# Cached keys laid out feature-major by the host, split straight from SBUF instead of transposed on TensorE

## The chip, the cores and the metric

The kernel runs on one core of one Trainium2 chip. The metric is the device time of one launch in microseconds (us). The profiled execution is one launch taken by the hardware profiler; its rows give times on the engines: PE (TensorE matmuls), PEld (weight loads of TensorE), DVE (VectorE), ACT (ScalarE), POOL (GpSimd) and SP (SyncE, which here only issues DMAs).

## The reference

One step of a one-layer hybrid encoder, for a prompt of 2048 tokens and for 8 batches of 16 new tokens with cached state. A combined projection feeds three branches (forgetting attention "fox" with 8 heads of 64, retention, and attention into 256 memory tokens with 4 heads of 128), which are gated, projected and merged. The change touches how the cached keys of the 8 batches enter the scores:

```python
PAST_LEN, DEC_BATCH, DEC_SEQ = 2048, 8, 16
# cache_fox_k (1, 8, 2048, 8, 64), cache_mem_k (1, 8, 256, 4, 128)
def fox_attend(q, c_q, q_pos, k, v, c_k):
    s = jnp.einsum('bqhd,bkhd->bhqk', q, k) * (DH_FOX ** -0.5)
    s = s + jnp.swapaxes(c_q, 1, 2)[..., :, None] - jnp.swapaxes(c_k, 1, 2)[..., None, :]
    s = jnp.where(k_pos[None, :] <= q_pos[:, None], s, -jnp.inf)
    p = jax.nn.softmax(s, axis=-1)
    return jnp.einsum('bhqk,bkhd->bqhd', p, v)
def memory_attend(q, mk, mv):
    s = jnp.einsum('bthd,bmhd->bhtm', q, mk) * (DH_MEM ** -0.5)
    return jnp.einsum('bhtm,bmhd->bthd', jax.nn.softmax(s, axis=-1), mv)
```

## The kernel before

Every fp32 operand of a matmul is split into a rounded part `h` and a rest `l`, both of a type that TensorE takes in one pass, and a product is three matmuls (`mm3`: h*h, h*l, l*h). The helper `split` does it with one cast on ACT (line 202) and one subtraction on DVE (line 205):

```python
S.copy(h, src)
V.tensor_tensor(l, src, f32(h), ALU.subtract)
```

The program has a long projection (to about 1700 us), then two lanes woven together, then the output blocks (from about 2850 us). The right lane does the prompt's retention and then the prompt's fox attention. The left lane does the memory attention of the prompt (`mem_prompt`), of the 8 batches (`decode_mem`), the fox attention of the 8 batches (`decode_fox`) and the first output block. Both lanes are generators, and `weave` and `paced` mix them in a fixed ratio as the program is written out; a scheduler with a model of each instruction's time then settles the order on each engine. On the chip every engine works its list off in that order, and SP issues all loads and stores from a single queue, so an instruction that waits holds up those behind it on its engine.

The prompt's fox attention runs beside everything that is told here. For a block of 128 queries and up to 512 keys, PE makes scores in `sc` (lines 1315 to 1318), DVE takes the maximum `f_mx` (1322), ACT the exponential `pt` (1323), POOL scales `pt` (1327) by a factor `f_f` that DVE makes (1247), PE transposes `pt` into the PSUM tile `tp` (1349), ACT and DVE split that into `ph` and `pl`, and PE multiplies with the values into `ov` (1367, 1368).

`decode_fox` takes one batch at a time (`unit(b)`), two batches overlapping. A batch has four score blocks (`ci`, 512 keys each) and one for the 16 new keys. In each of the four, SP loads two pieces `dkt` of 512 KB: keys on the partitions, 512 features in a row. For each group `g4` of 128 features PE transposes four 128x128 pieces of them into a bank of `tp` (line 1487), `split` makes `dkh` and `dkl` from that bank, and three matmuls add to the scores `ys`. So a batch has 64 transposes and 16 splits of 512 columns, all 8 have 512 and 128. Buffers: three of `dkt`, three of `dkh` and of `dkl`; the three banks of `tp` are shared with the prompt's attention. The cached values `dvt` are split by POOL alone (`dvh` line 1529, `dvl` line 1530) and multiplied into `ym`.

`decode_mem` does the same on a small scale: per batch one load `mkt` of 512 KB, 16 transposes (line 1646), two splits into `mkh` and `mkl`, and 12 matmuls into `ys`; the values are split by ACT (`mvh`) and POOL (`mvl`). It runs beside the end of retention, which loads a state `st` for each batch, splits it into `sth` and `stl`, and stores it back.

Of the kernel before, what the change touches and what calls it, by code (L numbers as in the profile page):

```python
# [9 lines left out]
F32 = mybir.dt.float32  # L10
# [9 lines left out]
P = 128  # L20
# [3 lines left out]
NB, TS = 8, 16  # L24
# [48 lines left out]
def body(ctx: ExitStack, tc: tile.TileContext, a, o, stop=99):  # L73
# [25 lines left out]
    def ptp(dt=F32):  # L99
        return ps["tp"].tile([P, 512], dt, name="tp")  # L100
# [10 lines left out]
    def pdt(dt=F32):  # L111
        return ps["tp"].tile([P, 512], dt, name="tp")
# [70 lines left out]
    def dma(out, in_):  # L183
        nc.sync.dma_start(out, in_)
# [1207 lines left out]
    def decode_fox(dp, dw):  # L1392
# [56 lines left out]
        def unit(b):  # L1449
# [17 lines left out]
            kv = a["cache_fox_k"][b].rearrange("(p j) c -> p j c", p=P)  # L1467
# [7 lines left out]
            for ci in range(5):  # L1475
                sc = pys()
                if ci < 4:
                    w = 512
                    kts = []
                    for j in range(2):  # L1480
                        kt = dw.tile([P, 2, 512], F32, name="dkt", bufs=3)
                        dma(kt, kv[:, 4 * ci + 2 * j:4 * ci + 2 * j + 2])
                        kts += [kt[:, 0], kt[:, 1]]
                    for g4 in range(4):
                        p = pdt()
                        for j in range(4):
                            T.transpose(p[:, j * P:(j + 1) * P], kts[j][:, g4 * P:(g4 + 1) * P], ident)
                        kh = dw.tile([P, 512], F32R, name="dkh", bufs=3)
                        kl = dw.tile([P, 512], F32R, name="dkl", bufs=3)
                        split(kh, kl, p)  # L1490
                        mm3(sc, qb[0][:, g4], qb[1][:, g4], kh, kl, g4 == 0, False)
                    T.matmul(sc, selr[32 * ci:32 * ci + 16], crow[32 * ci:32 * ci + 16], start=False, stop=True)
                else:
                    w = 16
                    bs = slice(b * TS, (b + 1) * TS)
                    for g4 in range(4):
                        mm3(sc[:, :16], qb[0][:, g4], qb[1][:, g4], ks[0][:, g4, bs], ks[1][:, g4, bs], g4 == 0, False)
                    T.matmul(sc[:, :16], selr[:16], cnT[:, bs], start=False, stop=False)
                    T.matmul(sc[:, :16], identb, dmask, start=False, stop=True)
# [114 lines left out]
    def decode_mem(dp, dw):  # L1614
# [14 lines left out]
        def unit(b):  # L1629
            bs = slice(b * TS, (b + 1) * TS)  # L1630
            kt = dw.tile([P, 2, 512], F32, name="mkt")
            vt = dw.tile([P, 2, 512], F32, name="mvt")
            dma(kt, a["cache_mem_k"][b].rearrange("(m p) c -> p m c", p=P))
# [6 lines left out]
            parts = []  # L1640
            for h2 in range(2):
                p = ptp()
                for hh in range(2):
                    for m in range(2):
                        h = 2 * h2 + hh
                        T.transpose(p[:, (2 * hh + m) * P:(2 * hh + m + 1) * P], kt[:, m, h * P:(h + 1) * P], ident)
                kh = dw.tile([P, 512], F32R, name="mkh", bufs=3)
                kl = dw.tile([P, 512], F32R, name="mkl", bufs=3)
                split(kh, kl, p)
                parts.append((kh, kl))  # L1650
# [6 lines left out]
            for h in range(4):  # L1657
                kh, kl = parts[h // 2]
                c = slice((h % 2) * 256, (h % 2 + 1) * 256)
                mm3(sc[:64, :256], qb[0][:, h], qb[1][:, h], kh[:, c], kl[:, c], h == 0, h == 3)  # L1660
# [149 lines left out]
def _layout(i):  # L1810
# [6 lines left out]
        "cache_fox_k": i["cache_fox_k"].reshape(NB, PAST, 512), "cache_fox_v": i["cache_fox_v"].reshape(NB, PAST, 512),  # L1817
        "cache_fox_logf": i["cache_fox_logf"].reshape(NB, PAST, 8), "state_ret": i["state_ret"].reshape(NB, 4, 128, 256),
        "cache_mem_k": i["cache_mem_k"].reshape(NB, NMEM, 512), "cache_mem_v": i["cache_mem_v"].reshape(NB, NMEM, 512),
# [25 lines left out]
```

## Time and profile before

| what | us |
|---|---|
| median of 3 runs | 3419.86 (3412.14 to 3420.2) |
| the profiled execution | 3407.82 |
| span of its trace | 3406.0 |
| busy in the span: PE, DVE, ACT, POOL | 3197.8, 2261.2, 1744.3, 1218.8 |
| decode_mem, first to last key transpose | 1967.5 to 2010.3 |
| decode_fox, first to last key transpose | 2075.3 to 2670.8 |

The profiled execution lies 12 us below the median of the runs. Busy times of PE are counted with the latency of each matmul, so a share near 100% means that PE always had something in work, not that it worked at its peak. A duration of a DMA issue on SP is the issue alone, not the transfer.

### The profile page before, as it was taken

What the parts mean: (1) busy time and instruction counts of PE and PEld (TensorE: products, weight loads), DVE (VectorE), ACT (ScalarE), POOL (GpSimd) and SP (SyncE); (2) the same over time, 40 slices, a digit from 0 to 9 for tenths busy, and PEclk for the clock granted to TensorE, in tenths of its full rate; (3) what the DMA queues carried; (4) which work ended last, traced back from release to release, by engine and by line L of the source; (5) the groups of instructions that cost most, each with busy time, mean ns of one, the idle gap of its engine ahead of it and who ended that gap; (6) DMA issues with size and microseconds to landing.
All of it is one profiled execution on the core that took longest, in us unless ns stands there. A gap on an engine that the chain in (4) does not pass through costs nothing.

```text
span 3406.0 us, 60265 instructions
## 1 busy us (share of the span) xinstructions
PE 3197.8 (94%) x22299; PEld 3000.5 (88%) x22299; DVE 2261.2 (66%) x3732; ACT 1744.3 (51%) x3404; POOL 1218.8 (36%) x1122
## 2 busy tenths in 40 slices
PE   6999999999999999999878888999999988999999
PEld 5998999999999999999878766878888888888899
DVE  7676676665565666565578877877777876545444
ACT  4453444555444555445478755767766764223222
POOL 4436444110220010220177444777777853100100
PEclk8999999999999999999989888999999999999999
DMA  4776565568557667667567766445655447676665
GB/s 168 229 253 202 172 209 192 193 208 254 171 166 215 203 212 244 204 187 220 194 207 218 244 199 176 148 149 161 188 177 167 121 139 226 187 220 202 184 192 161
DMA packets 628219, 660.94 MB, mean 194 GB/s; under 512 B 46060, under 2 KB 549252, under 8 KB 627860
## 3 DMA queue, kind: packets, MB, share of 16 engines
q1 hardware_dynamic: 627924, 657.08, 62.5%
q8 instruction: 176, 2.88, 0.3%
q14 instruction: 119, 0.97, 0.1%
HBM read 477.52 MB, written 179.41 MB: 193 GB/s over the span
## 4 chain that ended last, share of the span: by engine, by line
PE 67%; DVE 11%; DMA 10%; ACT 5%; issue 4%; POOL 3%; SPq 1%; DVEq 0%; ACTq 0%; POOLq 0%
PE a L443 7%; PE a L445 7%; PE a L444 7%; PE b L443 5%; PE b L445 5%; PE b L444 5%; PE tp L1349 3%; DMA out_y_p<-x 2%; DMA x<-in_x_prompt 2%; PE sc L1315 2%; PE ov L1368 2%; DVE wl L394 2%; PE tp L227 1%; PE tp L228 1%; PE tp L226 1%
## 5 line engine op out<-in xcount | busy, mean ns | idle before, releaser
L394 DVE TENSOR_TENSOR wl<-wr,wh 128x1024 fp32r<-128x1024 f32 (+1 forms) x386 | 570.0, 1480 | 286.5 <-ACT wh L393 281.0
L393 ACT CAST wh<-wr 128x1024 fp32r<-128x1024 f32 (+1 forms) x386 | 404.6, 1050 | 307.8 <-PE b L445 127.4
L443 PE MATMUL a<-wh,ho 128*128 128x256 f32 (+1 forms) x1432 | 407.2, 285 | 16.6 <-ACT gz L701 9.8
L444 PE MATMUL a<-wl,ho 128*128 128x256 f32 (+1 forms) x1432 | 405.4, 283 | 5.8 <-DVE wl L394 5.8
L445 PE MATMUL a<-wh,ho 128*128 128x256 f32 (+1 forms) x1432 | 406.0, 284 | 0.6 <-DVE ho L270 0.6
L221 ACT CAST wh<-wraw 128x1024 fp32r<-128x1024 f32 x120 | 123.2, 1049 | 344.1 <-DMA wraw<-in_w_p 139.1
L422 POOL TENSOR_TENSOR wr<-wr 128x1024 f32<-128x1024 f32 (+1 forms) x72 | 201.6, 2800 | 272.9 <-DMA wr<-in_w_in 237.7
L443 PE MATMUL b<-wh,ho 128*128 128x256 f32 (+1 forms) x1032 | 291.8, 283 | 5.3 <-ACT wh L393 2.1
L445 PE MATMUL b<-wh,ho 128*128 128x256 f32 (+1 forms) x1032 | 291.0, 283 | 5.4 <-DVE ho L270 5.4
L444 PE MATMUL b<-wl,ho 128*128 128x256 f32 (+1 forms) x1032 | 290.9, 282 | 0.5 <-DVE wl L394 0.5
L443 PEld LDWEIGHTS a<-wh,ho 128*128 128x128 f32 x1432 | 272.5, 190 | 20.3 <-ACT gz L701 11.8
L444 PEld LDWEIGHTS a<-wl,ho 128*128 128x128 f32 x1432 | 272.5, 190 | 6.3 <-DVE wl L394 6.3
L445 PEld LDWEIGHTS a<-wh,ho 128*128 128x128 f32 x1432 | 272.6, 190 | 1.2 <-DVE ho L270 1.2
L443 PE MATMUL a<-ho,wh 128*128 128x384 f32 (+1 forms) x768 | 252.7, 329 | 1.8 <-ACT gz L701 1.8
L444 PE MATMUL a<-ho,wh 128*128 128x384 f32 (+1 forms) x768 | 252.9, 329 | 0.0
L445 PE MATMUL a<-ho,wl 128*128 128x384 f32 (+1 forms) x768 | 252.1, 329 | 0.0
L454 ACT COPY kp<-a 128x256 f32<-128x256 f32 (+3 forms) x384 | 153.2, 404 | 182.1 <-PE a L445 181.4
L1323 ACT ACTIVATE pt<-sc,f_mx 128x512 f32<-128x512 f32 (+2 forms) x320 | 201.1, 630 | 72.3 <-DVE f_mx L1322 42.1
L1327 POOL TENSOR_SCALAR pt<-pt,f_f,f_nm 128x512 f32<-128x512 f32 (+3 forms) x288 | 206.5, 737 | 80.2 <-DVE f_nm L1251 17.2
L1322 DVE TENSOR_REDUCE f_mx<-sc 128x1 f32<-128x512 f32 (+2 forms) x320 | 191.4, 603 | 41.0 <-PE sc L1318 21.9
L205 DVE TENSOR_TENSOR pl<-tp,ph 128x512 fp32r<-128x512 f32 (+2 forms) x352 | 193.0, 561 | 36.3 <-ACT ph L202 35.0
L1732 POOL TENSOR_TENSOR gm<-gm,gm 128x512 f32<-128x512 f32 (+2 forms) x40 | 46.2, 1155 | 450.8 <-DVE gm L1730 450.7
(431 smaller groups left out, 10042.6 us busy)
## 6 DMA issues: line engine op xcount, KB each, us to landing
wr<-in_w_in SPq DMA_DIRECT2D x170, 512.0 KB
wraw<-in_w_p SPq DMA_DIRECT2D x80, 512.0 KB
dkt<-in_cache_fox_k SPq DMA_DIRECT2D x64, 512.0 KB
dvt<-in_cache_fox_v SPq DMA_DIRECT2D x64, 512.0 KB
wr<-sum_gl SPq DMA_DIRECT2D x48, 512.0 KB
wraw<-in_w_out SPq DMA_DIRECT2D x40, 512.0 KB
gtd<-gz SPq DMA_DIRECT2D x96, 192.0 KB
gt<-gtd SPq DMA_DIRECT2D x24, 768.0 KB
```

The lines of the kernel that those rows point to most:

```text
L205: V.tensor_tensor(l, src, f32(h), ALU.subtract)
L221: S.copy(whv[:, i * hc:(i + 1) * hc], rv)
L393: S.copy(h, t)
L394: eng.tensor_tensor(l, t, f32(h), ALU.subtract)
L422: G.tensor_tensor(out, x, y, op)
L443: T.matmul(out, lh(c), rh(c), start=first and c == 0, stop=False, skip_group_check=True)
L444: T.matmul(out, lh(c), rl(c), start=False, stop=False, skip_group_check=True)
L445: T.matmul(out, ll(c), rh(c), start=False, stop=last and c == 3, skip_group_check=True)
L454: S.copy(t[nm], t["a"])
L1322: V.tensor_reduce(nmx[:, j, ci:ci + 1], sc[:, :w], AX.X, ALU.max, negate=True)
L1323: S.activation(pt[:, :w], sc[:, :w], AF.Exp, bias=nmx[:, j, ci:ci + 1], accum_out=l[:, j, ci:ci + 1])
L1327: G.tensor_scalar(pt, pt, fb, 0.5 if r is None else r[:, j:j + 1], ALU.mult, ALU.mult)
```

## The change

The host now hands over the cached fox keys with the features on the partitions, `(batch, group of 128 features, 128, 2048 keys)`, and the memory keys as `(batch, head, 128, 256 keys)`. The keys of a fox block are rearranged on the host so that a row of 512 holds the same keys, in the same order, as the transposed bank did. A piece `dkt` is now two feature groups of 512 keys, is split at once (1024 columns), and goes straight into six matmuls, three for each of its groups. The transposes of lines 1487 and 1646 are gone, with their use of `tp`. `dkt`, `dkh` and `dkl` have two buffers each (the last two of twice the size), `mkt` has one for two, and `mkh` and `mkl` have two of twice the size for three.

```diff
@@ -1464,7 +1464,7 @@
             nmx = sp.tile([P, 1, 5], F32, name="d_mx")
             l = sp.tile([P, 1, 5], F32, name="d_l")
             f = sp.tile([P, 1, 5], F32, name="d_f")
-            kv = a["cache_fox_k"][b].rearrange("(p j) c -> p j c", p=P)
+            kv = a["cache_fox_k"][b].rearrange("g p k -> p g k")
             vvw = a["cache_fox_v"][b].rearrange("(p j) c -> p j c", p=P)
             crow = dw.tile([P, 512], F32R, name="crow")
             for ci in range(4):
@@ -1476,19 +1476,15 @@
                 sc = pys()
                 if ci < 4:
                     w = 512
-                    kts = []
-                    for j in range(2):
-                        kt = dw.tile([P, 2, 512], F32, name="dkt", bufs=3)
-                        dma(kt, kv[:, 4 * ci + 2 * j:4 * ci + 2 * j + 2])
-                        kts += [kt[:, 0], kt[:, 1]]
-                    for g4 in range(4):
-                        p = pdt()
-                        for j in range(4):
-                            T.transpose(p[:, j * P:(j + 1) * P], kts[j][:, g4 * P:(g4 + 1) * P], ident)
-                        kh = dw.tile([P, 512], F32R, name="dkh", bufs=3)
-                        kl = dw.tile([P, 512], F32R, name="dkl", bufs=3)
-                        split(kh, kl, p)
-                        mm3(sc, qb[0][:, g4], qb[1][:, g4], kh, kl, g4 == 0, False)
+                    for g2 in range(2):
+                        kt = dw.tile([P, 2, 512], F32, name="dkt")
+                        dma(kt, kv[:, 2 * g2:2 * g2 + 2, ci * 512:(ci + 1) * 512])
+                        kh = dw.tile([P, 2, 512], F32R, name="dkh")
+                        kl = dw.tile([P, 2, 512], F32R, name="dkl")
+                        split(kh, kl, kt)
+                        for g in range(2):
+                            g4 = 2 * g2 + g
+                            mm3(sc, qb[0][:, g4], qb[1][:, g4], kh[:, g], kl[:, g], g4 == 0, False)
                     T.matmul(sc, selr[32 * ci:32 * ci + 16], crow[32 * ci:32 * ci + 16], start=False, stop=True)
                 else:
                     w = 16
@@ -1628,26 +1624,18 @@
 
         def unit(b):
             bs = slice(b * TS, (b + 1) * TS)
-            kt = dw.tile([P, 2, 512], F32, name="mkt")
+            kt = dw.tile([P, 4, 256], F32, name="mkt", bufs=1)
             vt = dw.tile([P, 2, 512], F32, name="mvt")
-            dma(kt, a["cache_mem_k"][b].rearrange("(m p) c -> p m c", p=P))
+            dma(kt, a["cache_mem_k"][b].rearrange("h p m -> p h m"))
             dma(vt, a["cache_mem_v"][b].rearrange("(m p) c -> p m c", p=P))
             qb = []
             for src, zp in zip(qms, qblk):
                 z = zp[b % 2]
                 G.tensor_copy(z[:, :, 0:TS], f32(src)[:, :, bs])
                 qb.append(z.rearrange("p h c -> p (h c)")[:, :256].rearrange("p (h c) -> p h c", h=4))
-            parts = []
-            for h2 in range(2):
-                p = ptp()
-                for hh in range(2):
-                    for m in range(2):
-                        h = 2 * h2 + hh
-                        T.transpose(p[:, (2 * hh + m) * P:(2 * hh + m + 1) * P], kt[:, m, h * P:(h + 1) * P], ident)
-                kh = dw.tile([P, 512], F32R, name="mkh", bufs=3)
-                kl = dw.tile([P, 512], F32R, name="mkl", bufs=3)
-                split(kh, kl, p)
-                parts.append((kh, kl))
+            kh = dw.tile([P, 4, 256], F32R, name="mkh")
+            kl = dw.tile([P, 4, 256], F32R, name="mkl")
+            split(kh, kl, kt)
             vh = dw.tile([P, 2, 512], F32R, name="mvh")
             vl = dw.tile([P, 2, 512], F32R, name="mvl")
             S.copy(vh, vt)
@@ -1655,9 +1643,7 @@
             yield
             sc = pys()
             for h in range(4):
-                kh, kl = parts[h // 2]
-                c = slice((h % 2) * 256, (h % 2 + 1) * 256)
-                mm3(sc[:64, :256], qb[0][:, h], qb[1][:, h], kh[:, c], kl[:, c], h == 0, h == 3)
+                mm3(sc[:64, :256], qb[0][:, h], qb[1][:, h], kh[:, h], kl[:, h], h == 0, h == 3)
             mx = sp.tile([64, 1], F32, name="dm_mx")
             l = sp.tile([64, 1], F32, name="dm_l")
             V.tensor_reduce(mx, sc[:64, :256], AX.X, ALU.max, negate=True)
@@ -1814,9 +1800,10 @@
     ins = {
         "x_prompt": i["x_prompt"].reshape(SEQ, D), "x_sample": i["x_sample"].reshape(P, D),
         "mem_prompt": i["mem_prompt"].reshape(NMEM, D),
-        "cache_fox_k": i["cache_fox_k"].reshape(NB, PAST, 512), "cache_fox_v": i["cache_fox_v"].reshape(NB, PAST, 512),
+
+        "cache_fox_k": i["cache_fox_k"].reshape(NB, P, 16, 4, P).transpose(0, 3, 4, 2, 1).reshape(NB, 4, P, PAST), "cache_fox_v": i["cache_fox_v"].reshape(NB, PAST, 512),
         "cache_fox_logf": i["cache_fox_logf"].reshape(NB, PAST, 8), "state_ret": i["state_ret"].reshape(NB, 4, 128, 256),
-        "cache_mem_k": i["cache_mem_k"].reshape(NB, NMEM, 512), "cache_mem_v": i["cache_mem_v"].reshape(NB, NMEM, 512),
+        "cache_mem_k": i["cache_mem_k"].reshape(NB, NMEM, 4, P).transpose(0, 2, 3, 1), "cache_mem_v": i["cache_mem_v"].reshape(NB, NMEM, 512),
         "g_norm": i["g_norm"].reshape(D), "g_mem_norm": i["g_mem_norm"].reshape(D), "w_in": i["w_in"][0],
         "b_f": i["b_f"].reshape(8), "b_merge": i["b_merge"].reshape(24, P), "g_fox_q": i["g_fox_q"].reshape(64),
         "g_fox_k": i["g_fox_k"].reshape(64), "g_mem_q": i["g_mem_q"].reshape(128), "g_mem_k": i["g_mem_k"].reshape(128),
```

The scheduler makes its order anew from the first memory key on. On PE, in the second score block of the first batch of `decode_fox` (of the two `qb` the first is the rounded part of the queries, the second the rest), the kernel before has the transposes of one group between the matmuls of another:

```order
L227 MATMUL ys<-dkl,qb_23418 128x512
L228 MATMUL ys<-dkh,qb_23419 128x512
L226 MATMUL ys<-dkh,qb_23418 128x512
L1487 MATMUL tp<-kc,dkt 128x128 x4
L227 MATMUL ys<-dkl,qb_23418 128x512
L228 MATMUL ys<-dkh,qb_23419 128x512
L226 MATMUL ys<-dkh,qb_23418 128x512
L1349 MATMUL tp<-kc,pt 128x128 x4
L1367 MATMUL ov<-ph,vv 128x256
L1368 MATMUL ov<-pl,vv 128x256
L1367 MATMUL ov<-ph,vv 128x256
```

The changed kernel, in the second block of the same batch:

```order
L226 MATMUL ys<-dkh,qb_23306 128x512
L227 MATMUL ys<-dkl,qb_23306 128x512
L228 MATMUL ys<-dkh,qb_23307 128x512
L226 MATMUL ys<-dkh,qb_23306 128x512
L227 MATMUL ys<-dkl,qb_23306 128x512
L228 MATMUL ys<-dkh,qb_23307 128x512
L1488 MATMUL ys<-crow,selr 128x512
L1367 MATMUL ov<-ph,vv 128x256
L1315 MATMUL sc<-ka,qa 128x512
L1316 MATMUL sc<-kb,qb 128x512
L1368 MATMUL ov<-pl,vv 128x256
L1367 MATMUL ov<-ph,vv 128x256
```

The `tp<-kc,dkt` rows are gone, and all twelve matmuls of a block (the last six are shown) stand in a row; the prompt's instructions (`sc`, `ov`, `tp<-kc,pt`), which stood between them, come behind.

On DVE, at the first score block of the second batch, the kernel before has these rows (`f_mx` and `pl` belong to the prompt's attention, `d_mx` is the maximum of a score block):

```order
L205 TENSOR_TENSOR dkl<-tp,dkh 128x512
L1322 TENSOR_REDUCE f_mx<-sc 128x1
L205 TENSOR_TENSOR dkl<-tp,dkh 128x512 x2
L1322 TENSOR_REDUCE f_mx<-sc 128x1
L205 TENSOR_TENSOR dkl<-tp,dkh 128x512
L1322 TENSOR_REDUCE f_mx<-sc 128x1
L205 TENSOR_TENSOR pl<-tp,ph 128x512
L205 TENSOR_TENSOR pl<-tp,ph 128x256
L1500 TENSOR_REDUCE d_mx<-ys 128x1
```

The changed kernel, at the same block:

```order
L1322 TENSOR_REDUCE f_mx<-sc 128x1
L205 TENSOR_TENSOR dkl<-dkt,dkh 128x1024
L1496 TENSOR_REDUCE d_mx<-ys 128x1
L205 TENSOR_TENSOR dkl<-dkt,dkh 128x1024
L1322 TENSOR_REDUCE f_mx<-sc 128x1
L205 TENSOR_TENSOR pl<-tp,ph 128x512
L1440 COPY cq<-tp 128x8
L1322 TENSOR_REDUCE f_mx<-sc 128x1
L205 TENSOR_TENSOR pl<-tp,ph 128x512
L1496 TENSOR_REDUCE d_mx<-ys 128x1
```

Four subtractions of 512 columns out of `tp` became two of 1024 columns out of `dkt`, with the prompt's `f_mx` and `pl` queued behind them; they stand earlier too, ahead of the last `d_mx` of the batch before.

## Rows read from the trace of the kernel before

**Rows 1.** The page: busy us, share of the span, instructions.
```profile
PE 3197.8 (94%) x22299; PEld 3000.5 (88%) x22299; DVE 2261.2 (66%) x3732; ACT 1744.3 (51%) x3404; POOL 1218.8 (36%) x1122
```

**Rows 2.** Table by stretches: window, length, busy of each engine, clock, DMA.
```profile
2075.00:2675.00 600.00, 576.48 (x4029) 495.75 (x4029) 465.38 (x1015) 419.38 (x1102) 430.64 (x567) 0.99 0.54 161
1967.00:2016.00 49.00, 42.57 (x299) 36.81 (x298) 42.98 (x120) 26.64 (x56) 26.57 (x26) 0.95 0.71 234
1021.80:1107.00 85.20, 85.20 (x528) 85.13 (x526) 44.71 (x61) 40.60 (x65) 0.00 (x0) 1.00 0.71 216
255.45:340.60 85.15, 77.59 (x505) 76.31 (x504) 58.34 (x53) 31.55 (x50) 51.70 (x21) 0.94 0.63 202
```

**Rows 3.** The chain by line, from 2075 to 2675, then 1967 to 2016.
```profile
by line: PE tp L1349 13.4%; PE ov L1368 7.4%; PE sc L1315 7.2%; PE ov L1367 7.0%; PE tp L1487 6.8%; PE sc L1316 6.2%; PE ys L227 5.5%; PE ys L228 4.8%; PE ys L226 4.8%; PE ym L1534 4.3%; PE ym L1535 4.0%; DVE f_mx L1322 2.9%; issue 2.1%; AC
...
by line: DVE stl L205 9.4%; DVE mkl L205 8.6%; issue 8.0%; PE tp L1646 7.5%; PE ys L227 6.4%; PE ys L228 4.8%; PE tp L1678 4.8%; DVE gv L1077 4.6%; PE ys L226 4.3%; PE tp L1679 3.8%; PE tp L1686 3.7%; DVE mpt L1667 3.5%; DVE dm_mx L1663 3.0
```

**Rows 4.** Groups of instructions from 2075 to 2675: count, busy, mean ns, waits.
```profile
L1530 POOL TENSOR_TENSOR dvl<-dvt,dvh 128x512 fp32r<-128x512 f32 x113 | 143.5, 1289 | 0.6
...
L205 DVE TENSOR_TENSOR dkl<-tp,dkh 128x512 fp32r<-128x512 f32 x128 | 85.9, 684 | 37.0 <-ACT dkh L202 36.6
...
L1487 PE MATMUL tp<-kc,dkt 128*128 128x128 f32 x512 | 77.3, 277 | 0.0
L202 ACT CAST dkh<-tp 128x512 fp32r<-128x512 f32 x128 | 73.3, 589 | 59.9 <-PE tp L1487 57.2 <-PE ov L1367 0.8
...
L227 PE MATMUL ys<-dkl,qb 128*128 128x512 f32 x128 | 56.3, 440 | 8.5 <-DVE dkl L205 8.4
...
L1247 DVE TENSOR_TENSOR f_f<-f_nm,f_mx 128x8 f32<-128x8 f32 (+2 forms) x35 | 19.8, 566 | 0.9
```

**Rows 5.** The chain in order of time, near 2311: start, us, what.
```profile
2311.56 0.23 PE ys L226
2311.79 0.44 PE tp L1487 x4
```

**Rows 6.** The page: the weight cast of 1024 columns.
```profile
L221 ACT CAST wh<-wraw 128x1024 fp32r<-128x1024 f32 x120 | 123.2, 1049 | 344.1 <-DMA wraw<-in_w_p 139.1
```

**Rows 7.** Instructions of the tile dkl, then of line 1247: ns min/median/max.
```profile
L205 DVE TENSOR_TENSOR dkl<-tp,dkh x128: 670/681/693, 2077.1 to 2671.9; 128x512 fp32r<-128x512 f32 x128
...
L1247 DVE TENSOR_TENSOR f_f<-f_nm,f_mx x48: 153/186/6811, 2037.4 to 2813.8; 128x4 f32<-128x4 f32 x16, 128x6 f32<-128x6 f32 x16, 128x8 f32<-128x8 f32 x16
```

**Rows 8.** Groups of line 394 on DVE, 1021.8 to 1107, then 255.45 to 340.6.
```profile
L394 DVE TENSOR_TENSOR wl<-wr,wh 128x1024 fp32r<-128x1024 f32 x19 | 23.2, 1223 | 16.3 <-ACT wh L393 16.2
...
L394 DVE TENSOR_TENSOR wl<-wr,wh 128x1024 fp32r<-128x1024 f32 x16 | 35.6, 2231 | 16.5 <-ACT wh L393 16.4
```

**Rows 9.** Instructions in order of time, 2274 to 2283: DVE, then POOL.
```profile
2275.05 6.81 DVE L1247 TENSOR_TENSOR f_f<-f_nm,f_mx 128x6 f32<-128x6 f32 x1
...
2274.54 1.20 POOL L1529 TENSOR_SCALAR dvh<-dvt 128x512 fp32r<-128x512 f32 x2
2275.72 1.28 POOL L1530 TENSOR_TENSOR dvl<-dvt,dvh 128x512 fp32r<-128x512 f32 x1
2276.97 1.20 POOL L1529 TENSOR_SCALAR dvh<-dvt 128x512 fp32r<-128x512 f32 x2
2278.14 3.70 POOL L1530 TENSOR_TENSOR dvl<-dvt,dvh 128x512 fp32r<-128x512 f32 x3
```

**Rows 10.** Groups of instructions from 1967 to 2016.
```profile
L205 DVE TENSOR_TENSOR mkl<-tp,mkh 128x512 fp32r<-128x512 f32 x16 | 10.6, 676 | 3.2 <-ACT mkh L202 3.2
...
L205 DVE TENSOR_TENSOR stl<-st,sth 128x512 fp32r<-128x512 f32 x6 | 6.7, 1110 | 0.8 <-ACT sth L202 0.8
```

**Rows 11.** What SP's queue waited for: us in total, times, longest.
```profile
SPq L184 <- PE tp L1487: 63.7, 37, 11.3
```

**Rows 12.** The chain in order of time, 2753 to 2848: loads of 512 KB.
```profile
2753.28 7.24 DMA wraw<-in_w_p
...
2827.81 3.90 DMA wraw<-in_w_p
```

## Prediction

> **What bounds the kernel now.** I read the busy times of the page first: PE is busy 3197.8 of 3406.0 us, and DVE, the next, 2261.2 [rows 1]. The change touches two stretches only, so the table by stretches comes next [rows 2]. From 2075 to 2675 us the cached fox keys are scored beside the prompt's attention: PE is busy 576 of 600 us at a granted clock of 0.99, DVE 465, POOL 431, ACT 419. From 1967 to 2016 us the memory keys are scored beside the end of retention: PE 42.6 of 49 us, DVE 43.0, so no engine stands out there. What an edit is worth shows in the chain that ended last. In the first stretch that chain spends 6.8% in the key transposes of L1487; in the second 7.5% in those of L1646 and 8.6% in the subtraction that makes mkl [rows 3]. So the first stretch is bound by PE's order, with short visits to the others, and the second by latency, back and forth between engines.
>
> **The removed transposes.** PE issues 512 of them for the fox keys [rows 4]. Their mean of 277 ns is a latency; in the chain's own steps a group of four takes 0.44 us, where a 512-column score matmul takes 0.23 us [rows 5]. 128 groups x 0.44 = 56.3 us is the upper bound. The lower is what the chain holds: 6.8% of 600 = 40.8 us; in the other 15.5 us the chain was on another engine, and PE would have waited in any case. I take 40.8. For the memory keys the same two readings are 16 groups x 0.44 = 7.0 us, and 7.5% of 49 = 3.7 us; I take 3.7. Both together: -44.5 us, at most -63.3.
>
> **The splits.** ACT cast 128 pieces of 512 columns from PSUM at 589 ns, 75.4 us, ahead of which it waited 57.2 us for PE [rows 4]. Now it casts 64 pieces of 1024 columns from SBUF; the weight cast of that size takes 1049 ns [rows 6], so 67.1 us. ACT is 30% idle: nothing on the path.
>
> DVE is where the change may give time back. Before, the subtraction read one operand from PSUM and one from SBUF. All 128 took 670 to 693 ns [rows 7], though POOL was busy 72% of the time beside them [rows 2]. Now both operands lie in SBUF. The same form at the same size is the weight split of L394: 1223 ns in a stretch where POOL did nothing, and 2231 ns in one where POOL was busy 51.7 of 85.2 us [rows 2, 8]. So POOL's work can delay a DVE instruction that reads two SBUF tiles by 1.01 us. How it looks beside the fox keys is shown by f_f: a few columns, 153 ns at least [rows 7], 566 ns on average [rows 4], and once 6.81 us, from 2275.05 to 2281.86, where POOL's unbroken run of dvh and dvl ends at 2281.84 [rows 9]. DVE was not let in between POOL's instructions.
>
> The Trainium skill has the rule for it ("SBUF — State Buffer", section "Who interferes with whom"): a DVE instruction with two SBUF inputs contends with a GpSimd instruction that reads SBUF, whichever starts first holds the port for its whole instruction, and a DVE instruction with one SBUF input does not contend. The trace agrees [rows 7, 8, 9], and goes further: that wait went over a whole run of POOL instructions, not to the end of one. By the rule alone, as an estimate, a wait would be half a POOL instruction of 0.6 to 1.3 us in 72% of the cases, some 0.3 us, and the sum below -32 us.
>
> The wait per subtraction, from rows: f_f's mean less its least is 0.41 us; in the memory stretch a 512-column subtraction from SBUF, stl, took 1110 ns where one from PSUM, mkl, took 676 ns, so 0.43 us more [rows 10]; L394's 1.01 us is the upper bound, zero the lower. I take 0.5, near the rows of these two stretches. The new subtraction then takes 1.22 + 0.5 = 1.72 us, 64 of them 110 us against 85.9 us [rows 4]: +24 us on DVE, which goes from 78% to some 85% busy. I put half of it on the path, 12 us: a piece can be split ahead of its use, but behind each subtraction on DVE wait f_mx and pl of the prompt's attention, and for those ACT and PE. Bounds: 0, and with 1.01 us 64 x 2.23 - 85.9 = 57 us.
>
> The lock holds the other way too. While DVE subtracts, POOL stands still: 64 x 1.22 x 72% = 56 us, covered by 169 us in which POOL was idle. If that cover is gone, dvl (1289 ns each [rows 4]) and the scaled pt come late, and PE waits before ym and tp. I put 5 us on the path; bounds 0 and 56.
>
> For the memory keys there are 8 subtractions of 1.22 + 0.43 = 1.65 us, 13 us, for 16 x 0.676 = 10.8 us, in a stretch where the chain runs through them: +2 us.
>
> **Loads and buffers.** The 64 fox key loads stay 512 KB each, in runs of 2 KB for 4 KB. dkt has two buffers for three, and a buffer comes free when DVE has subtracted, no longer when PE has transposed; SP's wait for that was 63.7 us in 37 times [rows 11], with the prompt's q, k and gate loads behind it in SP's queue. mkt has one buffer for two, so its next load waits for mkl, and loads of st for retention wait behind it. A 512 KB load on the chain took 3.9 to 7.2 us [rows 12]. In PE's order the changed kernel does the first score block of a batch some 200 rows ahead of the other three, and these three 21 to 51 rows apart; before, the four stood 49 to 110 rows apart. So the third and fourth block need their keys in quick succession. I put 0 on the path: cast and subtraction of a piece stand ahead of the block before, and PE does the prompt's attention meanwhile. The bound is one spread of landings, 3.3 us, at three blocks of each of 8 batches: 80 us.
>
> **The sum.** -40.8 - 3.7 + 12 + 5 + 2 = -25.5 us. Against the profiled execution, 3407.8 us, that is 3382 us. The median of the runs shown is 12 us higher, 3419.9, so I forecast 3394 us, 0.75% less. Under 0.3%, about 10 us, a measurement of this kernel can't tell from no change.
>
> **The rivals.** (1) All PE slots come back and nothing is paid: -63.3 us, 3357 us. For it speaks PE's 576 of 600 us, and that the three tp banks get freer for the prompt's attention; against it, that the chain holds only 44.5 of the 63.3. (2) The port between DVE and POOL takes the gain. POOL's 431 us and DVE's 78 unblocked us are 509 us of a stretch of 575: 89% of the time someone holds it. With DVE's 24 us, a third of POOL's 56 us and the 2 us all on the path, the 44.5 us are gone: 3420 us. Late key loads, at 8 of the 24 blocks by 3.3 us each, would take the forecast's 25.5 us as well. (3) Slower, by one mechanism: DVE's subtraction is shut out until POOL's run of dvh and dvl ends, as f_f was, and the prompt's f_mx and pl stand behind it. With all of that on the path the gain is gone at 0.82 us of wait per subtraction (44.5 + 7.8 us, the latter what 64 unblocked ones save, over 64). At L394's 1.01 us, and a quarter of POOL's 56 us with it, it is -44.5 + 57 + 14 + 2 = +28 us: 3448 us. For it: the 6.81 us; against: f_f waits 0.41 us on average beside the same POOL. That the transposes stay is excluded: PE's order holds none of them.
>
> **Chances.** The forecast 0.47, (1) 0.20, (2) 0.17, (3) 0.16: faster 0.67, same 0.17, slower 0.16. The forecast by itself spans 3377 (DVE's and POOL's waits both hidden) to 3406 (DVE's 24 us all on the path). The range takes in (1), (2) and about half of (3): 3354 to 3432.
>
> **What would show it.** No tp<-kc,dkt on PE; 64 of dkl<-dkt,dkh with a mean near 1.7 us and a tail of several us that ends with POOL's runs. A mean near 1.2 us speaks for (1), above 2.2 us for (3). What PE's matmuls of dkl waited, 8.5 us before [rows 4], should rise to 10 to 20 us, and dvl should lengthen from 1289 ns. The stretch of the fox key scores should shrink by some 20 us, the memory stretch by 2. If waits for the loads of dkt lead PE's list, putting 0 for the loads was the mistake; if the stretch shrinks as said and the end does not move, something behind it gave the time back.

## The result, and the profile after

The changed kernel takes 3442.68 us (median of 4 runs, 3438.37 to 3455.67) against 3417.84 us for the kernel before: ratio 1.0079, 95% interval 1.0055 to 1.0104. It is slower by 0.8%, 25 us, where 0.75% less was forecast, and 11 us above the range. The two profiled executions, 3407.82 and 3446.45 us, differ by more, 38.6 us, since the one of before lies 10 us under its median and the one of after 4 us over its own. Nearly all of it stands in one stage: from the first score matmul of the prompt's attention (`sc`) to its last `ov`, 832.3 us became 871.1 us.

The page's busy line of the changed kernel, to [rows 1], then the table by stretches, to [rows 2]:

```profile
PE 3176.4 (92%) x21723; PEld 2973.2 (86%) x21723; DVE 2310.4 (67%) x3660; ACT 1743.4 (51%) x3332; POOL 1257.2 (36%) x1122
```

```profile
2075.00:2675.00 600.00, 524.37 (x3294) 440.28 (x3294) 481.61 (x902) 391.43 (x973) 432.53 (x526) 0.92 0.51 151
1967.00:2016.00 49.00, 37.65 (x220) 32.22 (x219) 41.86 (x103) 23.70 (x44) 28.86 (x25) 0.85 0.68 214
```

PE has less to do (576.48 to 524.37 us busy of the same 600) and no other engine is near full, yet the stretch gets through less: 120 of the 128 groups' matmuls lie in it. PE's granted clock fell from 0.99 to 0.92. The chain by line over the stretch, to [rows 3], shows who ends last instead. In this trace the chain can be followed back only to 2256 us, so its shares are of 600 us though it covers some 419 of them:

```profile
by line: DVE dkl L205 4.9%; PE tp L1349 4.7%; issue 4.5%; DMA dkt<-in_cache_fox_k 4.2%; PE sc L1315 3.4%; DVE f_mx L1322 3.3%; DVE pl L205 3.2%; PE ov L1368 3.0%; PE sc L1316 2.8%; DVE f_f L1247 2.8%; PE ov L1367 2.8%; PE ys L226 2.2%; PE y
```

Before, 71.4% of that chain were eleven lines of PE and 2.9% `f_mx`. The shares of the two can't be compared as they stand, but their ranks can: now the subtraction `dkl` is the longest line (4.9% of 600 is 29 us, 7% of what is covered), and the loads of `dkt` (25 us), `f_mx`, `pl` and `f_f` stand among the lines of PE. The groups of the stretch, to [rows 4], and the tile `dkl`, to [rows 7] (numbers: least/median/most, ns), with its group over the whole trace:

```profile
L1526 POOL TENSOR_TENSOR dvl<-dvt,dvh 128x512 fp32r<-128x512 f32 x103 | 138.7, 1367 | 0.6
...
L205 DVE TENSOR_TENSOR dkl<-dkt,dkh 128x1024 fp32r<-128x1024 f32 x59 | 102.7, 1741 | 28.9 <-ACT dkh L202 28.9
...
L202 ACT CAST dkh<-dkt 128x1024 fp32r<-128x1024 f32 x59 | 61.6, 1051 | 34.9 <-DMA dkt<-in_cache_fox_k 12.8 <-PE ys L228 10.7 <-PE ov L1368 3.7
...
L227 PE MATMUL ys<-dkl,qb 128*128 128x512 f32 x120 | 51.5, 429 | 5.2 <-DVE dkl L205 5.2
...
L1247 DVE TENSOR_TENSOR f_f<-f_nm,f_mx 128x6 f32<-128x6 f32 (+2 forms) x32 | 26.7, 835 | 0.6
```

```profile
L205 DVE TENSOR_TENSOR dkl<-dkt,dkh x64: 1204/1332/8042, 2054.7 to 2678.4; 128x1024 fp32r<-128x1024 f32 x64
...
L205 DVE TENSOR_TENSOR dkl<-dkt,dkh 128x1024 fp32r<-128x1024 f32 x64 | 109.1, 1704 | 29.4 <-ACT dkh L202 29.3
```

The new subtraction takes 1704 ns on average over all 64 (109.1 us; 1741 ns for those in the stretch), as forecast, but its median is 1332 ns: most lose little and a few are shut out for up to 8 us. The waits of the stretch (total us, times, longest), of the changed kernel and then of the kernel before:

```profile
ACT pt L1323 <- DVE f_mx L1322: 56.8, 64, 6.6
POOL pt L1327 <- DVE f_nm L1251: 40.4, 11, 8.9
...
PE ov L1368 <- DVE pl L205: 24.1, 14, 5.6
...
ACT dkh L202 <- DMA dkt<-in_cache_fox_k: 12.8, 10, 2.1
...
PE ys L227 <- DVE dkl L205: 5.2, 2, 3.8
```

```profile
ACT pt L1323 <- DVE f_mx L1322: 23.9, 42, 3.2
...
POOL pt L1327 <- DVE f_nm L1251: 9.8, 5, 2.8
...
PE ov L1368 <- DVE pl L205: 2.3, 3, 1.1
```

PE hardly waits for `dkl` itself: 5.2 us, 8.4 before, where the prediction's sign was a rise to 10 to 20 us. The wait passes through the prompt's attention: ACT for `f_mx` 56.8 us (23.9), POOL for DVE's `f_nm` 40.4 (9.8), PE for `pl` 24.1 (2.3). One such stop, in order of time on DVE, POOL and SP, then the chain there, and the stretch by windows:

```profile
2415.93 0.69 DVE L1496 TENSOR_REDUCE d_mx<-ys 128x1 f32<-128x512 f32 x1 [0.31 <-PE ys L1488]
2416.54 7.50 DVE L205 TENSOR_TENSOR dkl<-dkt,dkh 128x1024 fp32r<-128x1024 f32 x1
2423.97 0.68 DVE L1322 TENSOR_REDUCE f_mx<-sc 128x1 f32<-128x512 f32 x1
...
2425.70 0.68 DVE L205 TENSOR_TENSOR pl<-tp,ph 128x512 fp32r<-128x512 f32 x1
```

```profile
2413.91 2.94 POOL L1327 TENSOR_SCALAR pt<-pt,f_f,f_nm 128x512 f32<-128x512 f32 x4
2416.81 2.53 POOL L1526 TENSOR_TENSOR dvl<-dvt,dvh 128x512 fp32r<-128x512 f32 x2
2419.30 1.22 POOL L1525 TENSOR_SCALAR dvh<-dvt 128x512 fp32r<-128x512 f32 x2
2420.47 2.49 POOL L1526 TENSOR_TENSOR dvl<-dvt,dvh 128x512 fp32r<-128x512 f32 x2
```

```profile
2410.73 0.59 SPq L184 DMA_DIRECT2D fg<-fgd  x1
2424.07 2.12 SPq L184 DMA_DIRECT2D dkt<-in_cache_fox_k  x2
```

```profile
2415.24 0.23 PE ys L228
...
2416.54 7.51 DVE dkl L205
...
2424.89 0.43 PE ys L228
```

```profile
2404.00:2416.00 12.00, 12.00 (x82) 9.63 (x82) 9.40 (x22) 10.44 (x27) 6.55 (x9) 1.00 0.31 84
2416.00:2424.00 8.00, 4.27 (x31) 3.69 (x31) 8.00 (x3) 2.06 (x4) 6.96 (x8) 0.89 0.00 0
2424.00:2430.00 6.00, 5.90 (x15) 4.37 (x15) 5.80 (x10) 3.88 (x9) 0.00 (x0) 0.58 0.63 193
2430.00:2440.00 10.00, 10.00 (x76) 9.39 (x76) 7.38 (x14) 7.09 (x18) 7.09 (x7) 1.00 0.80 263
```

`dkl` is due at 2416.54 and ends at 2424.04, 1.08 us after POOL's run of `pt`, `dvl`, `dvh`, `dvl` (ended 2422.96): its own work, done behind the whole run. `f_mx` stands behind it. SP issues nothing from 2411.3 on, 12.7 us long, because its next load needs the `dkt` buffer that this subtraction frees, so the share of the DMA engines falls to 0.00. PE runs dry (4.27 us busy of 8), and then gets a mean clock of 0.58 over 6 us, in which most 512-column matmuls take 0.43 us for 0.23. The Trainium skill ("SBUF — State Buffer", "Who interferes with whom") lets whoever issues first hold the shared port for its whole instruction; this row agrees that DVE is fully blocked, but through a run of instructions.

### The profile page after: what moved, and what is told of

It is laid out like the page before. It is cut to its first block, busy times and chain, and to the rows that moved or that the text cites. A ratio compares the mean times of both kernels' runs of the same rounds, so it can differ in the third digit from the quotient of the medians.

```text
span 3444.3 us, 59088 instructions
## 1 busy us (share of the span) xinstructions
PE 3176.4 (92%) x21723; PEld 2973.2 (86%) x21723; DVE 2310.4 (67%) x3660; ACT 1743.4 (51%) x3332; POOL 1257.2 (36%) x1122
## 5 line engine op out<-in xcount | busy, mean ns | idle before, releaser
L1327 POOL TENSOR_SCALAR pt<-pt,f_f,f_nm 128x512 f32<-128x512 f32 (+3 forms) x288 | 216.8, 767 | 84.2 <-DVE f_nm L1251 52.5
```

What stands on the lines that cost most here:

```text
L1327: G.tensor_scalar(pt, pt, fb, 0.5 if r is None else r[:, j:j + 1], ALU.mult, ALU.mult)
```

## The experiments

Ratios are to the kernel before, measured beside each on the same chip, with the 95% interval. In all of them the scheduler makes its order anew, which the fourth group prices.

**What is PE's time worth?** `e10_zero_matmuls` puts two matmuls with a zero operand behind each group's three:

```diff
...
                             mm3(sc, qb[0][:, g4], qb[1][:, g4], kh[:, g], kl[:, g], g4 == 0, False)
+                            T.matmul(sc, zq, kh[:, g], start=False, stop=False)
+                            T.matmul(sc, zq, kh[:, g], start=False, stop=False)
```

> The changed kernel with two more matmuls by a zero operand for every group of a score block, 256 x 0.23 = 59 us of work for PE, nothing else. If PE's time is still what sets the stage, it goes up by 40 to 60 us, to 3480 to 3505 us. If PE has slack (theory C), by less than 15 us: 3435 to 3458 us, with a higher granted clock from 2100 to 2675 us than the 0.93 of the changed kernel.

It took 3451.19 us, a ratio of 1.0109 (1.0093 to 1.0125). Its stretch (the windows' columns):

```profile
2075.00:2675.00 600.00, 565.67 (x3556) 477.96 (x3554) 460.93 (x903) 394.05 (x978) 436.39 (x533) 0.96 0.51 153
```

256 matmuls at the chain's 0.23 us [rows 5] are 59 us, as much as the transposes took, and they cost 8.5 us, 0.3%, over the changed kernel. In the changed kernel PE has room for them, and with them its clock is 0.96 for 0.92: PE's work alone doesn't set that kernel's time. Whether the kernel before had such room is not shown by this; there PE was busy 576 of 600 us. No run put the zero matmuls into the kernel before, or left out its transposes and nothing else; the pairs below bear on it.

**The port.** `e1_before_sbuf_sub`: the kernel before, whose subtraction reads a second SBUF tile (the queries) for the bank of `tp`; by that it leaves out the true rest of the keys of the 8 batches.

```diff
-                        split(kh, kl, p)
+                        S.copy(kh, p)
+                        V.tensor_tensor(kl, f32(qs[0]).rearrange("p g t -> p (g t)"), f32(kh), ALU.subtract)
```

> The kernel before with its transposes, pieces and buffers, except that the fox key subtraction on DVE reads a second SBUF tile of the same 128x512 (the queries of the stage) where it read the transposed PSUM bank, so dkl holds a wrong rest and the scores of the 8 batches are off. The score blocks stand as far apart in PE's order as before. Theory A (the lock between DVE and POOL): the 128 subtractions rise from 0.684 us to 1.0 to 1.2 us, the prompt's f_mx comes late, and the time is 3430 to 3470 us. Theory B (the blocks of a batch stand too close together since the tp banks no longer hold them back, and loads and splits come in bursts): no blocks moved, so 3408 to 3428 us.

It took 3422.43 us, 1.0003 (0.9986 to 1.0020), not told from no change, where the theory of the port expected 3430 or more. `e2_after_psum_sub` is the changed kernel with a copy on ACT from which DVE subtracts, so with one operand in PSUM; `e9_act_copy_sbuf_sub` is the same with `kt[:, g]` for `p` in the subtraction, all else equal:

```diff
-                        split(kh, kl, kt)
+                        S.copy(kh, kt)
+                        for g in range(2):
+                            p = pdt()
+                            S.copy(p, kt[:, g])
+                            V.tensor_tensor(kl[:, g], p, f32(kh)[:, g], ALU.subtract)
```

> The changed kernel, but ACT also copies each 512 columns of dkt into a tp bank, and DVE subtracts from there, 512 columns at a time: one SBUF input. No transposes, 128 more ACT copies of about 0.59 us, 75 us. The score blocks stand as far apart as in the kernel before. Theory A: dkl takes 0.68 us each as before, PE has its 40 us back, less some 10 us for ACT: 3375 to 3400 us. Theory B expects the same, since the bursts are gone too. If it is above 3425 us, both are wrong and the transposes on PE cost nothing.

> The second experiment again (ACT copies 512 columns of each piece into a bank of tp, the splits are of 512 columns), but the subtraction reads both operands from SBUF. Its pair took 3433 us with 681 ns per subtraction. Port (DVE shut out by POOL is what costs): the 128 subtractions go from 87 us to some 130 us, as they did in the kernel before with an SBUF operand (1049 ns each), and the time rises by 20 us or more, 3453 to 3475. Bursts and late loads: no change from the pair, 3427 to 3439. POOL and the prompt's path as the bound, with PE waiting: the port costs what it takes from POOL, 128 x 0.55 us x 70% = 49 us of holding, of which I expect a quarter on the path, 3440 to 3450.

They took 3433.24 us, 1.0043 (1.0026 to 1.0060), and 3453.85 us, 1.0100 (1.0076 to 1.0125). The tile `dkl` in the three, for `e1` with its group:

```profile
L1491 DVE TENSOR_TENSOR dkl<-dq,dkh x128: 666/814/5281, 2079.6 to 2695.5; 128x512 fp32r<-128x512 f32 x128
...
L1491 DVE TENSOR_TENSOR dkl<-dq,dkh 128x512 fp32r<-128x512 f32 x128 | 132.3, 1049 | 19.4 <-ACT dkh L1490 18.6
```

```profile
L1488 DVE TENSOR_TENSOR dkl<-tp,dkh x128: 659/681/693, 2078.5 to 2703.1; 128x512 fp32r<-128x512 f32 x128
```

```profile
L1488 DVE TENSOR_TENSOR dkl<-dkt,dkh x128: 669/728/7926, 2054.0 to 2701.5; 128x512 fp32r<-128x512 f32 x128
```

With one operand in PSUM there is no tail at all, with two in SBUF it reaches 5 and 8 us; nothing else in that instruction differs. Between `e2` and `e9` the tail goes with 20 us. In `e1` it goes with nothing, though the subtractions take 132.3 us for 85.9 [rows 4]: DVE's waits have no fixed price in time. And without any tail `e2` is still no faster than the kernel before, and over the 3425 us above which its expectation held both theories wrong: the transposes are gone there, but ACT's copies are new, and ACT's waits for the loads of `dkt` are 46.2 us (12.8 in the changed kernel), so it doesn't price the transposes alone.

**POOL's part.** `e5_before_nodvl` and `e6_after_nodvl` are the two kernels with the values' rest set to zero instead of subtracted (left out: that part of the values), so POOL works less and reads less.

```diff
-                                G.tensor_tensor(vl[:, i], vt[:, i], f32(vh)[:, i], ALU.subtract)
+                                G.memset(f32(vl)[:, i], 0.0)
```

> The kernel before, with POOL setting the rest of the cached values, dvl, to zero instead of subtracting: the low part of the values is left out, and POOL reads less SBUF. It is the control for the same edit in the changed kernel. Both theories: DVE's subtraction of the keys reads one SBUF input, so only f_f and the like get shorter and POOL gets freer: 3395 to 3418 us.

> The changed kernel with dvl set to zero by POOL, as in the control: the low part of the values is left out. The score blocks stand as close as in the changed kernel. Theory A: POOL holds the port some 140 us less, dkl falls from 1.72 us to 1.4 us or less, and the gap to the control closes: 3375 to 3410 us, not above the control. Theory B: the bursts stay, so it is 20 us or more above the control: 3415 to 3440 us.

They took 3383.41 us, 0.9891 (0.9869 to 0.9913), and 3374.17 us, 0.9866 (0.9834 to 0.9897): 34.7 us less for the kernel before, 68.5 us for the changed one. `dkl` in `e6`, then the stretch in `e5` and `e6`:

```profile
L205 DVE TENSOR_TENSOR dkl<-dkt,dkh x64: 1206/1226/1703, 2054.4 to 2612.6; 128x1024 fp32r<-128x1024 f32 x64
```

```profile
2075.00:2675.00 600.00, 583.18 (x4140) 505.26 (x4140) 463.21 (x1047) 431.24 (x1141) 355.58 (x587) 1.00 0.52 162
```

```profile
2075.00:2675.00 600.00, 572.54 (x3765) 492.09 (x3763) 472.46 (x1035) 438.84 (x1102) 389.52 (x602) 0.95 0.56 167
```

No subtraction takes over 1.71 us now, and the changed kernel is 9 us below its control (the two intervals overlap, so this is not told from nothing), where with POOL's reads it is 25 us above. POOL's relief alone gives the control its 34.7 us, where 3395 us or more was expected. `e19_after_act_dvh` keeps all the work: the changed kernel with `dvh` made by ACT.

```diff
-                                G.tensor_scalar(vh[:, i], vt[:, i], 1.0, 1.0, ALU.mult, ALU.mult)
+                                S.copy(vh[:, i], vt[:, i])
```

> The changed kernel, its keys split in pieces of 1024 columns as there, with dvh made by ACT for POOL. POOL loses some 80 us, and no longer has unbroken runs of value splits; ACT goes from 560 to some 635 us of the stage. If POOL, and DVE shut out behind its runs, is what the changed kernel pays for: 25 to 45 us under the changed kernel, 3398 to 3418, with a subtraction under 1.55 us on average. If ACT's exponentials come late for it: 3435 to 3460.

It took 3396.10 us, 0.9939 (0.9923 to 0.9955), 47 us under the changed kernel. Its stretch and its `dkl` there:

```profile
2075.00:2675.00 600.00, 553.58 (x3578) 468.81 (x3578) 472.21 (x973) 469.55 (x1163) 393.42 (x460) 0.95 0.54 160
```

```profile
L205 DVE TENSOR_TENSOR dkl<-dkt,dkh 128x1024 fp32r<-128x1024 f32 x60 | 86.8, 1449 | 23.1 <-ACT dkh L202 22.2 <-DMA ka<-ktH 0.4
```

ACT gained 78 us in the stretch and POOL lost 39, and it is faster, so ACT has room. How much of the 47 us is POOL's own time and how much what DVE meets there is not parted: the kernel before with ACT's `dvh` was not run, and `e5` shows that relief of POOL alone can be worth 34.7 us.

**Pieces, buffers, order.** `e3_small_pieces` splits 512 columns at a time, with three buffers of `dkt`, `dkh`, `dkl` as before; `e12_small_two_buffers` is the same with two of `dkt` and four of the half-size `dkh` and `dkl` (shown), the changed kernel's SBUF.

```diff
-                        kh = dw.tile([P, 2, 512], F32R, name="dkh")
-                        kl = dw.tile([P, 2, 512], F32R, name="dkl")
-                        split(kh, kl, kt)
                         for g in range(2):
...
+                            kh = dw.tile([P, 512], F32R, name="dkh", bufs=4)
+                            kl = dw.tile([P, 512], F32R, name="dkl", bufs=4)
+                            split(kh, kl, kt[:, g])
...
```

> The changed kernel with pieces and buffers as before: splits of 512 columns, three buffers of dkt, dkh and dkl. Same bytes read from SBUF by DVE. Theory A: 128 subtractions wait as the control with an SBUF operand showed (0.81 us at the median), the time stays within 15 us of the changed kernel, 3428 to 3458 us. Theory B (loads come late for two buffers): 20 us faster or more, 3400 to 3424 us, and the waits of dkh for the loads of dkt, 17.8 us, go away.

> The changed kernel with splits of 512 columns for 1024 and nothing else: dkt has two buffers as in the changed kernel, dkh and dkl four of half the size, the same SBUF. The run with three buffers of each gave 3416 us. If the third load buffer gave that back (late loads): 3436 to 3446, with the wait of dkh for loads back at 10 us and more. If the size of the piece did (a shorter stop for f_mx and pl behind each subtraction, and a shorter hold of the port): 3412 to 3424, with 128 subtractions near 0.95 us. If both count by halves: 3424 to 3436.

They took 3416.41 us, 1.0004 (0.9990 to 1.0019), and 3418.26 us, 1.0002 (0.9986 to 1.0018). What ACT's `dkh` of `e12` waited for loads in the stretch, 12.8 us in the changed kernel:

```profile
ACT dkh L202 <- DMA dkt<-in_cache_fox_k: 21.3, 18, 2.8
```

That is more waiting for loads, and 24 us less time. In `e3`, with its third buffer, ACT has no such wait, and it is no faster. So ACT's waits for late loads don't set the time in these two kernels; more load buffers with pieces of 1024 columns were not run. `e7_fox_only` has the change for the fox keys and leaves the memory keys as before; against the changed kernel, in `decode_mem`:

```diff
-            kt = dw.tile([P, 4, 256], F32, name="mkt", bufs=1)
+            kt = dw.tile([P, 2, 512], F32, name="mkt")
...
+                        T.transpose(p[:, (2 * hh + m) * P:(2 * hh + m + 1) * P], kt[:, m, h * P:(h + 1) * P], ident)
```

> The changed kernel with the memory keys loaded, transposed and split as before. All theories: the memory keys are worth little, since the stretch up to the first fox score ended 3.6 us later in the changed kernel: 3432 to 3444 us. If it is under 3425 us, the memory part with its one buffer carries the loss.

It took 3417.71 us, 1.0021 (1.0007 to 1.0035), under the 3425 us below which its expectation put the loss on the memory keys. Before such differences are believed, order has to be priced. The last six change one number, the pace of the cached lane, which moves instructions on every engine and leaves the work alone: the changed kernel at 49 and 45, with 512-column splits at 49 and 45, the kernel before at 49 and 45. Their expectations in this order:

```diff
-                yield from paced(decode_fox(*pools(st, "left", ("dp", 1), ("dw", 2))), 47, 730)
+                yield from paced(decode_fox(*pools(st, "left", ("dp", 1), ("dw", 2))), 49, 730)
```

> The changed kernel with the pace of the cached lane at 49 steps for 47, the same work in a slightly other order on every engine. This measures what order alone does, and all theories expect the same: within 8 us of the changed kernel, 3435 to 3451. If it moves by 15 us or more, differences of that size between the variants (the smaller pieces, the change for the fox keys alone) cannot be put down to their edits.

> The changed kernel at a pace of 45 steps for the cached lane (47 in the changed kernel, 49 in the run before: 0.8% and 0.3% over the kernel before). If large pieces lose whatever the order: ratio 1.003 to 1.010. If the loss of the changed kernel is an accident of its order: 1.000 or less at one of the paces.

> Splits of 512 columns with two load buffers, at a pace of 49; its pair with 1024 columns had 1.0032. If the size of the piece decides: 0.995 to 1.000, some 15 to 24 us under its pair, as at the pace of 47. If order decides: within 8 us of its pair, 1.001 to 1.006.

> The same with 512 columns at a pace of 45. If the size of the piece decides: 15 to 24 us under the kernel with 1024 columns at the same pace; if order decides: within 8 us of it, or above.

> The kernel before at a pace of 49: what order does where the keys are transposed. If the kernel before has cover that the changed one lacks (its transposes are spread, POOL and DVE don't meet for the keys): within 5 us of itself, 0.9985 to 1.0015. If order is worth as much there: off by 8 us or more to either side.

> The kernel before at a pace of 45. With the runs at 47 and 49 this gives its spread by order. If it stands firm: 0.9985 to 1.0015. If order is worth as much as in the changed kernel: off by 8 us or more.

| ratio at a pace of | 45 | 47 | 49 |
|---|---|---|---|
| before | 1.0071 (1.0057 to 1.0084) | 1 | 0.9997 (0.9981 to 1.0012) |
| changed | 1.0065 (1.0045 to 1.0085) | 1.0079 (1.0055 to 1.0104) | 1.0032 (1.0017 to 1.0048) |
| changed, 512 columns | 1.0044 (1.0029 to 1.0059) | 1.0002 (0.9986 to 1.0018) | 1.0025 (1.0011 to 1.0039) |

Order alone moves the same work by up to 0.7%, 24 us. The change costs nothing at 45, 0.8% at 47 and 0.35% at 49, 0.4% or 12 us on average; a gain of 0.75% shows nowhere. The changed kernel at 49, expected within 8 us of itself at 47, is 16 us off. `e14` came out as large pieces that lose whatever the order would, but that mark is set against the kernel before at 47, which itself loses as much at 45 (`e18`). `e15` and `e16` lie 2 and 7 us under their pairs, as order would have it. The 512-column pieces take off 0.2%, 0.8% and 0.1%: at 45 and 49 the intervals don't tell them from 1024, so most of the 24 us at 47 is likely order. The longest stops do not go with the cost either. At a pace of 45, where the change costs nothing, `dkl` is:

```profile
L205 DVE TENSOR_TENSOR dkl<-dkt,dkh x64: 1205/1248/8000, 2053.4 to 2670.2; 128x1024 fp32r<-128x1024 f32 x64
```

The 0.6% by which `e7` lies under the changed kernel, the port's 20 us and the zero matmuls' 8.5 us lie inside this spread; the 35 to 68 us of `e5`, `e6` and `e19` lie outside it, as does the gap between 8.5 and 59 us. The runs of POOL's part were each made in one order only.

**Something better.** `e4_fp32_direct` doesn't split the keys: one fp32 matmul for each group, with the sum `qw` of the two parts of the queries and five buffers of `dkt`. `e11_fp32_act_dvh` has ACT's `dvh` as well (the edit of `e19`).

```diff
...
-                            mm3(sc, qb[0][:, g4], qb[1][:, g4], kh[:, g], kl[:, g], g4 == 0, False)
+                            T.matmul(sc, qw[:, g4], kt[:, g], start=g4 == 0, stop=False)
```

> The changed kernel, but the fox keys are not split: one fp32 matmul per group on dkt as it lands (its queries are the two parts added up), 128 matmuls in place of 384, five buffers of dkt. Neither ACT nor DVE touches the keys. An fp32 matmul of 512 columns stands in no row; bounds are the 0.23 us of one split matmul and four times that, 0.92 us, so PE spends 29 to 118 us for 88 us now. Theory A (what hurts is DVE's 1024-column subtraction against POOL's dvl): 3350 to 3390 us. Theory C (removing PE work buys nothing, since PE then waits for the prompt's chain and its granted clock falls): no lower than 3400 us.

> The unsplit keys (3404 us: one fp32 matmul for a group, no cast and no subtraction) with dvh made by ACT, 128 casts of 512 columns, in place of POOL. POOL loses some 78 us of 568 us, ACT gains some 75 us on 500 us. If POOL, with the scaled pt behind its value splits, is what sets the stage: 25 us and more off, 3370 to 3382. If PE or the loads set it: 3398 to 3408. If ACT takes over as the bound with its exponentials late: 3408 to 3425.

They took 3404.08 us, 0.9966 (0.9949 to 0.9982), and 3392.34 us, 0.9919 (0.9898 to 0.9940). The second is the best kernel here that does all the work, 0.8% under the kernel before, and lies between the ranges that its expectation named. In `e4` neither the transposes nor any split of the fox keys is left. In its chain a group costs PE two matmuls of 0.43 us, for 0.44 us of transposes and three matmuls of 0.23 us in the kernel before: as an estimate PE has 128 x 0.27 = 35 us less to do, 1.0%, and 0.3% came back. With no key subtraction on DVE, ACT's `dvh` brings 12 us; beside the subtractions it brought 47. That fits a cost of their meeting, with order's spread on both numbers.

## Why the prediction was wrong

- **The removed transposes, -40.8 us: the step that failed.** The chain's share on L1487 was taken for time that comes back. Nowhere did it come back: at three paces the change costs 0, 25 and 12 us, in the pair without POOL's reads it is worth 9 us, not 41, and `e2`, which has no tail on DVE (and costs of its own on ACT), is slower than the kernel before. As much PE work put into the changed kernel (`e10`) costs 8.5 us. PE's 576 of 600 us read as "bound by PE's order"; that the other engines fed it just in time, so that it could not run ahead, is argued and not shown. The clock is part of this by the rows, though no run isolates it: 0.99 to 0.92 of 600 us is, as an estimate, (0.07 / 0.5) x 600 = 84 us more at the half clock, up to 42 us of PE's work. Nothing of the clock stood in the sum.
- **The split's duration, 1.72 us: right** (1.704), and ACT's 67.1 us too (64 x 1051 ns = 67.3).
- **Half of DVE's 24 us on the path and 5 us for POOL: too little.** The two are one meeting: without POOL's reads of `dvl` the change gives -9 us, with them +25, so they are worth 34 us for the forecast's 17 (each difference with order's spread on it). That -9 + 34 is the 25 us measured holds by construction and checks nothing. That these stops cost this much is argued, not shown: in `e1` 46 us more of such waits cost nothing, and at a pace of 45 stops as long cost nothing. The mean hid the form: a few stops of several us, each with `f_mx`, `pl` and SP's loads behind it.
- **Loads and buffers, 0: borne out in part.** A third buffer brought nothing with 512-column pieces (`e3` against `e12`). In the changed kernel itself loads of `dkt` hold 25 us of the chain, one of them (4.19 us from 2668.42) right behind a `dkl` of 4.19 us, and no run parts the two.
- **Memory keys, -3.7 and +2 us: not settled.** The subtraction took 1.33 us, not 1.65, so the +2 us was not there; the rest lies inside order's spread.

```profile
L205 DVE TENSOR_TENSOR mkl<-mkt,mkh 128x1024 fp32r<-128x1024 f32 x7 | 9.3, 1333 | 2.3 <-ACT mkh L202 2.2
```

- **Rival (3)**, with 0.16, named what the trace shows: DVE shut out behind POOL's runs, the prompt's `f_mx` and `pl` behind it. That its 3448 us lies near the 3442.68 measured is luck: its price (2.23 us a subtraction) did not come. 1.70 us went with the loss, since the 44.5 us against it weren't there. Its condition, 0.82 us of wait, was worked out from that same -44.5. `f_f`, from which the wait was read, rose from 566 to 835 ns, and SP's wait for the `dkt` buffer from 63.7 [rows 11] to:

```profile
SPq L184 <- DVE dkl L205: 72.5, 27, 12.7
```

- **What the prediction had no term for is order.** The 25 us are the change at a pace of 47; the mean over three paces is 12 us, so about half of the loss, as far as three paces tell, is the order that the scheduler happened to make. What stays open is why one order does better than another, how the other half parts into DVE's stops, late loads and the clock, and what the transposes alone were worth in the kernel before.

## What to carry to other kernels

A busy engine that heads the chain is not yet a bound: before pricing removed work at the chain's share, run the kernel before without that work, or with as much idle work added, and see whether the time moves. Here the idle work went into the changed kernel alone, which tells of that kernel only. When an operand moves from PSUM to SBUF, look what POOL reads at that moment and how long its unbroken runs are: a stop lasts as long as the run, with all that queues behind it. Its price in time is another question (46 us of it cost nothing in `e1`). Relieving POOL was worth more here (35 and 47 us, each in one order) than leaving out the transposes. Where a scheduler rebuilds the order on every edit, time the same work in two or three orders first; here differences under 0.7% were not the edit's for certain.

## What the hardware showed that was not expected

A DVE subtraction with two SBUF operands was shut out over a whole run of POOL instructions of three kinds, 7.50 us for 1.20; in `e1` and `e9` single ones of 512 columns took 5.28 and 7.93 us for 0.67. With POOL's `dvl` turned into a fill, which reads nothing, the longest of 64 took 1.70 us; POOL's `dvh` and `pt` still read there, the former in runs that the fills break up. The Trainium skill ("SBUF — State Buffer", "Who interferes with whom") says that a GpSimd instruction that only writes does not contend with such a subtraction; the 1.70 us, beside 8.04 in the changed kernel, agree. TensorE's clock went to a mean of 0.58, so mostly its level of 1.2 GHz, over 6 us right after 8 us in which PE was busy 4.27, and was 1.00 again from 2430 to 2440 us; more work on PE (`e10`) raised the mean granted clock of the stretch from 0.92 to 0.96.
